# Sink heads: probabilities divided by VectorE ahead of their transposes, and the transposes around the values put in another order

## The chip, the cores and the metric

One core of a Trainium2 chip runs the whole kernel in one launch. The metric is the device time of one execution in microseconds (us). The core has a matmul engine (TensorE, PE in the profile, with its weight loads as PEld), three engines for elementwise work (VectorE or DVE, ScalarE or ACT, GpSimd or POOL) and a queue for transfers (SyncE, SP). They run side by side, each through its own list of instructions in order, and wait for each other by semaphores.

## The reference

Two layers over 256 tokens of width 1024, all in float32. Each layer is a half-weighted SwiGLU block, an attention block and a second half-weighted SwiGLU block. The attention block has two kinds of heads on one input projection. The A heads, with which the change deals, have a learned sink logit:

```python
m = jnp.maximum(jnp.max(scores, axis=-1, keepdims=True), sink_l)
e = jnp.exp(scores - m)
p = e / (jnp.sum(e, axis=-1, keepdims=True) + jnp.exp(sink_l - m))
out = jnp.einsum('bnkgqj,bnjkd->bnqkgd', p.astype(v.dtype), vb)
```

There are eight A query heads on two key heads; with 256 tokens and a window of 128 the band is written as a mask over all 256 keys. The four B heads are differential attention (one softmax less lambda times another) with a norm behind it, which takes any common factor out again. Both outputs go through one output projection.

## The kernel before

Everything is cut into tiles of 128 rows. Weights are read from memory as blocks of 1 MB, a few smaller (`raw`), and split by ScalarE and VectorE into a high and a low part in TensorE's rounded format (`w`: ScalarE copies, VectorE subtracts, `emit_split`, L207); a product is then three matmuls of 128x512: high by high, low by high, high by low (`tokens`). The order of splits relative to the matmuls is set by the numbers in `LEAD` (L32): at each place where the program takes the next block (`weights`, L273, and `ahead`, L244), a number says how many half blocks ahead of it are to be split by then. In the rest of the program the instructions stand as written (`Kept`, L52). In the softmax part of the attention (`kept[0] = False` at L1035 until L1157) the instructions of ScalarE, VectorE and GpSimd are put in order by the scheduler; TensorE's always stand as written, and `urgent` (L100) moves what it encloses forward.

PSUM has six banks for general use (`bank`, L83) and two for pairs (`pair`, L86; `xy` in the profile).

The attention is `mix` (L959). A step of it deals with two rows of heads at once; A steps are numbered 0 to 3 (two of the eight A heads each). `scores` (L986) does 24 short matmuls, then for each half of the queries and each head a VectorE step that adds the bias and takes the row's extremum (`negm`), and a ScalarE exponential with its row sum (`den`). `soft_b` (L1010) joins the two softmaxes of a B head. `soft_a` (L1023) adds the sink to the sum: `es`, its exponential, and `den_a`. It returns the exponentials undivided.

Then the program turns them keys-first: `keys_first` (L1053) does eight transposes on TensorE into two banks, and copies one bank by ScalarE, the other by VectorE. There are two groups for the B heads (`keys_first_b`) and four for the A heads (`keys_first_a`, one for each A step). The matmuls of the B values (`vB`, 48 of 128x512 in a pair of banks) are interleaved: the scores of A steps 0 and 1 behind kk = 1, those of steps 2 and 3 and the second B group behind kk = 4 (L1089). vB is scaled, half by ScalarE, half by VectorE, behind A group 0. Then come the A groups 1 to 3, and the B outputs (32 matmuls of `v` by `s`, into a pair, `osl`).

The A heads' divisor is applied last. The reciprocals of all sums (`ra`, L1105) are spread by GpSimd over 64 columns for each head (`rw`), transposed by TensorE four at a time (`turn_sums`, L1112), copied by ScalarE, and multiplied by VectorE into the output `oa`, which 16 matmuls of 64x256 have just made of the transposed exponentials and `vA`; the product `t_` is split into `oT` (L625). This happens twice (`cp`), for two groups of heads each. `norm_b` (L1129) brings the B outputs to the same form, and `out_part` multiplies `oT` by the output weights.

Of the kernel before, what the change touches and what calls it, by code (L numbers as in the profile page):

```python
# [9 lines left out]
F32 = mybir.dt.float32  # L10
F32R = mybir.dt.float32r
AF = mybir.ActivationFunctionType
ALU = mybir.AluOpType

P = 128
# [13 lines left out]
N_RAW, N_S4 = 6, 28  # L29
IN_FFN, IN_MIX = 8, 6  # L30
SEVEN = ((2, 3, 4), (1, 2, 3, 4))
LEAD = dict(start=(5, 7, 10, 10),  # L32
            open0=(2, 0, 0, 2, 6, 6, 8, 6, 5, 6, 1, 10, 2, 5, 7, 7, 8, 0),
            first=(1, 1, 1, 7, 12, 15, 16, 19, 19, 22, 22),
            mid=(2, 8, 12, 12, 15, 15, 20, 20, 20, 22, 23),
            last=(1, 7, 12, 14, 15, 15, 17, 20, 20, 21, 22),
            mid0=(6, 9, 12, 14, 15, 15, 19, 19, 19, 22, 24),
            last0=(2, 8, 12, 13, 15, 15, 19, 20, 20, 23, 25),
            first0=(2, 3, 3, 4, 7, 11, 11, 14, 14, 18, 18),
            open=(8, 12, 11, 9, 11, 11, 9, 5),  # L40
            close0=(7, 5, 7, 5, 6, 10, 3, 10, 5, 11, 4, 7, 1),
            close=(1, 8, 9, 9, 6, 8, 8, 9, 1, 7, 5, 4, 6),
            mix=(10, 2, 0, 2, 9, 2, 3, 5, 6, 11, 5, 2, 3, 1, 6, 5, 2, 4, 1, 6, 7, 8, 6, 11, 7, 8))


@with_exitstack
def trunk(ctx: ExitStack, tc: tile.TileContext, x, n1, g1, u1, d1, nm, w_in, sink,
# [21 lines left out]
    pe, act, dve, pool = Kept(nc.tensor, True), Kept(nc.scalar), Kept(nc.vector), Kept(nc.gpsimd)  # L69
# [30 lines left out]
    def urgent():  # L100

        return tc.high_priority(300)
# [402 lines left out]
    norm = Norm(0)  # L505

    def take_x(k):
# [15 lines left out]
        elif k == 1.25:  # L523
            norm.pair(2)
            norm.squares(1, 0, 512)
            ahead(LEAD["start"][0])
        elif k == 1.5:
# [157 lines left out]
    def ffn(norm, aside=None, before=None, final=False, sevens=SEVEN[1]):  # L685
# [57 lines left out]
        def by_sevens(h, groups, old):  # L743
# [215 lines left out]
    def mix(l, norm, nxt_norm):  # L959
        kbs = {}  # L960
        den_b = tmp("den_b", 1, (P, HB, 4))
        den_a = tmp("den_a", 1, (P, 4, 4))
# [60 lines left out]
        def soft_a(c, q):  # L1023
            ns = nsnk[:, l, c].rearrange("p t s -> p (t s)")
            den = den_a[:, c]
            e, negm = scores(q, kbs["a"], distA, [slopeA[c], slopeA[c + 4]], [ns[:, n:n + 1] for n in range(4)], den)
            es = tmp("es", 4, (P, 4))
            dve.tensor_tensor(es, negm, snk[:, l, c].rearrange("p t s -> p (t s)"), op=ALU.add)
            act.activation(es, es, AF.Exp)
            dve.tensor_tensor(den, den, es, op=ALU.add)  # L1030
            return e


# [12 lines left out]
        vsl = halves(bank())  # L1046
# [6 lines left out]
        def keys_first(pick):  # L1053

            out_ = blk(F32)
            for kc in range(2):
                tsl = bank()
                for i in range(4):
                    pe.transpose(tsl[:, i * P:(i + 1) * P], pick(kc, i), ident)
                (act.copy if kc == 0 else dve.tensor_copy)(out_[:, kc], tsl)  # L1060
            return out_

        def keys_first_b(hp):
            return keys_first(lambda kc, i: a_b[2 * hp + i // 2][:, i % 2, kc * P:(kc + 1) * P])

        def keys_first_a(c):
            return keys_first(lambda kc, i: p_a[c][:, i % 2, (i // 2) * 256 + kc * P:(i // 2) * 256 + (kc + 1) * P])


        aT = [keys_first_b(0)]  # L1070
        vB = tp.tile([P, 2, 512], F32, tag="v", bufs=1, name=nm_("v"))
        both = pair()
        vsl = both
        for k0 in (0, 4):
            w = weights()
            for k in range(4):
                kk = k0 + k
                hi, lo = w.part(k)
                xv = norm.xs[kk // 2][:, kk % 2]
                for t in range(2):  # L1080
                    xh, xl = xv[:, t * P:(t + 1) * P], xv[:, S + t * P:S + (t + 1) * P]
                    pe.matmul(vsl[t], lhsT=xh, rhs=hi, start=kk == 0, stop=False)
                    pe.matmul(vsl[t], lhsT=xl, rhs=hi, start=False, stop=False)
                    pe.matmul(vsl[t], lhsT=xh, rhs=lo, start=False, stop=kk == KC - 1)
                if kk == 1:
                    p_a = [soft_a(0, qA0[0]), soft_a(1, qA0[1])]
                elif kk == 4:
                    p_a += [soft_a(2, qA1[0]), soft_a(3, qA1[1])]
                    aT.append(keys_first_b(1))  # L1089
        pT = [keys_first_a(0)]  # L1090
        act.activation(vB[:, 0], vsl[0], AF.Copy, scale=norm.r[:, 0:1])
        dve.tensor_scalar_mul(vB[:, 1], vsl[1], norm.r[:, 1:2])
        for c in range(1, 4):
            pT.append(keys_first_a(c))

        def turned(o, cp, sl):

            for c in range(2):
                for t in range(2):
                    pe.transpose(sl[:, c * 256 + t * P:c * 256 + (t + 1) * P],  # L1100
                                 o[:, t, (2 * cp + c) * P:(2 * cp + c + 1) * P], ident)
            return halves(sl)


        ra = tmp("ra", 1, (P, 4, 4))  # L1105
        dve.reciprocal(ra, den_a)
        rw = blk(F32)
        for t in range(2):
            pool.tensor_copy(rw[:, t].rearrange("p (c a d) -> p c a d", c=4, a=2),
                             ra[:, :, 2 * t:2 * t + 2].unsqueeze(3).to_broadcast([P, 4, 2, 64]))  # L1110

        def turn_sums(cp):  # L1112
            turned(rw, cp, rsl[cp])
            rT = tmp()
            act.copy(rT, halves(rsl[cp]))
            return rT


        oT = [blk() for _ in range(4)]
        rsl, both = [bank() for _ in range(2)], pair()  # L1120
        osl = both
        for t in range(2):
            for h in range(HB):
                for kc in range(2):
                    c0 = (h % 2) * 256 + t * P
                    pe.matmul(osl[t][:, h * P:(h + 1) * P], lhsT=aT[h // 2][:, kc, c0:c0 + P],
                              rhs=vB[:, kc, h * P:(h + 1) * P], start=kc == 0, stop=kc == 1)

        def norm_b():  # L1129

# [28 lines left out]
        next(of_b)  # L1159
        oa = [halves(bank()) for _ in range(2)]  # L1160
        for cp in range(2):
            rT = turn_sums(cp)
            for c in range(2):
                for kc in range(2):
                    for a in range(2):
                        pp = slice(a * 64, a * 64 + 64)
                        pe.matmul(oa[cp][pp, c], lhsT=vA[:, kc, pp], rhs=pT[2 * cp + c][:, kc, a * 256:a * 256 + 256],
                                  start=kc == 0, stop=kc == 1)
            t_ = tmp()
            if cp:  # L1170
                next(of_b)
            dve.tensor_tensor(t_, oa[cp], rT, op=ALU.mult)
            split(oT[cp], t_)


        accs = [[bank(), bank()] for _ in range(2)]
# [35 lines left out]
    for l in range(DEPTH):  # L1212
# [7 lines left out]
        if not final:  # L1220
            norm = Norm((l + 1) * 8)
# [76 lines left out]
```

## Time and profile before

| what | before |
|---|---|
| median of three runs | 911.79 us (911.65 to 912.84) |
| the profiled execution | 912.2 us |
| its span, first to last instruction | 910.4 us |
| TensorE busy | 902.3 us |
| VectorE busy | 777.5 us |
| ScalarE busy | 613.8 us |
| granted TensorE clock, mean | 0.998 |
| attention of layer 0, A and B softmax to output projection | about 198 to 281 us of the span |
| attention of layer 1 | about 645 to 728 us |

The busy times are of the one profiled execution; the instructions of an engine overlap a little, so the differences of starts in a list by time are a better measure of what a group takes than the durations in it. In the profile nearly all lines read L62, since a helper there issues the instructions, and one goes by tiles: `ident,s` are transposes, `s,vA` the A outputs, `v,s` the B outputs, `w,s` products with weights.

### The profile page before, as it was taken

Reading aid. Unit: us, or ns where it says so; the run is one execution under the profiler, and the core shown is the slowest. Engines: PE = TensorE matmul, PEld = TensorE weight load, DVE = VectorE, ACT = ScalarE, POOL = GpSimd, SP = SyncE. Lnnn points to the kernel's source line nnn. Section 1 sums busy time; section 2 is a strip of 40 time slices with the busy share of each in tenths; the row PEclk is TensorE's granted clock in tenths of the full one; section 3 lists DMA queues with packets and bytes.
Section 4 is the critical chain, followed back from the end, with each engine's and each line's share of the span. In section 5 each row is a group of like instructions: output and inputs, shape, how many; then the busy total and the mean of one; then the engine's idle time right before and its main releaser. Section 6 shows DMA issues by size and latency. Waiting matters only on the chain.

```text
span 910.4 us, 12060 instructions
## 1 busy us (share of the span) xinstructions
PE 902.3 (99%) x4486; PEld 754.2 (83%) x4486; DVE 777.5 (85%) x1053; ACT 613.8 (67%) x975; POOL 64.9 (7%) x83
## 2 busy tenths in 40 slices
PE   9999999999999999999999999999999999999997
PEld 8888888888888888888888888888888888888886
DVE  5859999879876899999778999997896878999894
ACT  6856677677776766677575776676766686776660
POOL 0411000000001001000000101000001000101011
PEclk9999999999999999999999999999999999999999
DMA  9998897956048788897966898897720786898731
GB/s 331 336 271 235 232 317 249 266 141 224 1 145 236 176 269 247 239 306 249 304 186 163 254 282 265 238 303 214 219 98 1 256 215 176 235 311 250 222 114 47
DMA packets 114060, 200.83 MB, mean 221 GB/s; under 512 B 3663, under 2 KB 31377, under 8 KB 114001
## 3 DMA queue, kind: packets, MB, share of 16 engines
q1 hardware_dynamic: 97344, 167.53, 54.1%
q0 software_dynamic: 16096, 31.75, 20.1%
q8 instruction: 35, 0.57, 0.3%
q10 hardware_dynamic: 560, 0.79, 0.3%
q14 instruction: 25, 0.20, 0.1%
HBM read 199.00 MB, written 1.05 MB: 220 GB/s over the span
## 4 chain that ended last, share of the span: by engine, by line
PE 91%; DMA 5%; DVE 1%; ACT 1%; issue 1%; POOL 0%; SPq 0%; POOLq 0%; ACTq 0%
PE ps L62 69%; PE xy L62 22%; DMA raw<-in_ffn_w_up_dram 4%; DVE w L62 1%; DMA raw<-in_ffn_w_gate_dram 1%; ACT w L62 1%; ACT junk L62 0%; POOL r L62 0%; ACT s L62 0%; DVE s L62 0%; ACT tmp L62 0%; SPq L172 0%; DVE xk L62 0%; DVE q L62 0%; POOLq L1293 0%
## 5 line engine op out<-in xcount | busy, mean ns | idle before, releaser
L62 DVE TENSOR_TENSOR w<-raw,w 128x1024 fp32r<-128x1024 f32 (+1 forms) x458 | 476.7, 1099 | 36.1 <-ACT w L62 35.1
L62 PE MATMUL ps<-w,s 128*128 128x512 f32 (+1 forms) x2046 | 473.7, 389 | 0.3 <-DVE s L62 0.3
L62 ACT CAST w<-raw 128x1024 fp32r<-128x1024 f32 (+1 forms) x458 | 405.0, 953 | 60.6 <-DVE raw L62 40.9
L62 PEld LDWEIGHTS ps<-w,s 128*128 128x128 f32 x2046 | 380.2, 188 | 78.7 <-ACT tmp L62 0.8
L62 PE MATMUL xy<-w,s 128*128 128x512 f32 x528 | 125.7, 391 | 0.0
L62 PEld LDWEIGHTS xy<-w,s 128*128 128x128 f32 x528 | 98.3, 188 | 20.3
L62 PE MATMUL xy<-w,q 128*128 128x512 f32 x360 | 88.1, 393 | 0.0
L62 PEld LDWEIGHTS xy<-w,q 128*128 128x128 f32 x360 | 66.5, 188 | 13.2
L62 PE MATMUL ps<-s,w 128*128 128x512 f32 (+1 forms) x384 | 70.2, 339 | 0.0
L62 POOL DMA_DIRECT2D raw<-in_ffn_w_up_dram x30 | 38.9, 1315 | 432.6 <-DVE w L62 262.6
L62 DVE TENSOR_TENSOR raw<-raw,raw 128x2048 f32<-128x2048 f32 x30 | 68.7, 2289 | 0.5
L62 PEld LDWEIGHTS ps<-s,w 128*128 128x128 f32 x384 | 58.9, 188 | 8.4
L62 ACT ACTIVATE s<-ps,gcol 128x256 fp32r<-128x256 f32 (+1 forms) x80 | 31.4, 478 | 38.3 <-PE ps L62 38.3
L62 PE MATMUL ps<-w,q 128*128 128x512 f32 x180 | 43.2, 389 | 0.0
L62 PE MATMUL ps<-w,v 128*128 128x512 f32 x180 | 43.2, 389 | 0.0
L62 ACT CAST s<-ps 128x512 fp32r<-128x512 f32 x32 | 18.1, 593 | 36.5 <-PE ps L62 36.3
L62 PEld LDWEIGHTS ps<-w,q 128*128 128x128 f32 x180 | 33.8, 188 | 7.0
L62 PEld LDWEIGHTS ps<-w,v 128*128 128x128 f32 x180 | 33.8, 188 | 7.0
L62 DVE TENSOR_TENSOR s<-ps,s 128x512 fp32r<-128x512 f32 x32 | 21.3, 688 | 18.0 <-ACT s L62 17.9
L62 ACT ACTIVATE s<-s,negm 128x256 f32<-128x256 f32 x64 | 31.7, 498 | 6.1 <-DVE negm L62 6.0
L62 PE MATMUL ps<-ident,s 128*128 128x128 f32 x256 | 34.0, 273 | 0.0
L62 PEld LDWEIGHTS ps<-ident,s 128*128 128x128 f32 x256 | 29.7, 140 | 4.8 <-issue 0.8
(128 smaller groups left out, 557.2 us busy)
## 6 DMA issues: line engine op xcount, KB each, us to landing
raw<-in_ffn_w_down_dram SPq DMA_DIRECT2D x44, 1024.0 KB, 7.3
raw<-in_ffn_w_gate_dram SPq DMA_DIRECT2D x39, 1024.0 KB, 7.4
raw<-in_ffn_w_up_dram SPq DMA_DIRECT2D x39, 1024.0 KB, 7.1
raw<-in_ffn_w_up_dram POOLq DMA_DIRECT2D x30, 1024.0 KB, 9.8
raw<-in_w_in_dram SPq DMA_DIRECT2D x14, 1024.0 KB, 7.7
raw<-in_ffn_w_gate_dram SPq DMA_DIRECT2D x8, 512.0 KB, 8.0
raw<-in_ffn_w_up_dram SPq DMA_DIRECT2D x8, 512.0 KB, 9.0
raw<-in_w_in_dram SPq DMA_DIRECT2D x8, 512.0 KB, 6.8
```

The source lines that it names most:

```text
L62: ins = issue(*a, **k)
```

## The change

1. `soft_a` divides the exponentials itself: a reciprocal of the four sums of two heads (into `es`) and one VectorE product of 128x1024 with these four numbers broadcast along 256 columns each, in place.
2. `ra`, `rw`, `turn_sums` and the product with `rT` go away; `split` reads the A output in PSUM.
3. The second B group of transposes moves from behind kk = 4 to behind the last matmul of vB; vB's scaling becomes urgent and stands ahead of it; A groups 0 and 1 follow, then the B outputs, then A groups 2 and 3.
4. Ten of the twelve rows of `LEAD` change, in one to eighteen of their numbers each. One of these rows, and the rest of the diff:

```diff
-            mix=(10, 2, 0, 2, 9, 2, 3, 5, 6, 11, 5, 2, 3, 1, 6, 5, 2, 4, 1, 6, 7, 8, 6, 11, 7, 8))
+            mix=(10, 0, 0, 0, 11, 3, 2, 6, 8, 9, 5, 1, 3, 0, 3, 5, 2, 2, 4, 5, 4, 8, 1, 10, 4, 9))
...
             dve.tensor_tensor(den, den, es, op=ALU.add)
+            dve.reciprocal(es, den)
+            ev = e.rearrange("p t (a n) -> p (t a) n", a=2)
+            dve.tensor_tensor(ev, ev, es.unsqueeze(2).to_broadcast([P, 4, 256]), op=ALU.mult)
             return e
...
                     p_a += [soft_a(2, qA1[0]), soft_a(3, qA1[1])]
-                    aT.append(keys_first_b(1))
+        with urgent():
+            act.activation(vB[:, 0], vsl[0], AF.Copy, scale=norm.r[:, 0:1])
+            dve.tensor_scalar_mul(vB[:, 1], vsl[1], norm.r[:, 1:2])
+        aT.append(keys_first_b(1))
         pT = [keys_first_a(0)]
-        act.activation(vB[:, 0], vsl[0], AF.Copy, scale=norm.r[:, 0:1])
-        dve.tensor_scalar_mul(vB[:, 1], vsl[1], norm.r[:, 1:2])
-        for c in range(1, 4):
-            pT.append(keys_first_a(c))
+        pT.append(keys_first_a(1))
...
-        ra = tmp("ra", 1, (P, 4, 4))
-        dve.reciprocal(ra, den_a)
-        rw = blk(F32)
-        for t in range(2):
-            pool.tensor_copy(rw[:, t].rearrange("p (c a d) -> p c a d", c=4, a=2),
-                             ra[:, :, 2 * t:2 * t + 2].unsqueeze(3).to_broadcast([P, 4, 2, 64]))
-
-        def turn_sums(cp):
-            turned(rw, cp, rsl[cp])
-            rT = tmp()
-            act.copy(rT, halves(rsl[cp]))
-            return rT
...
+        for c in (2, 3):
+            pT.append(keys_first_a(c))
...
         for cp in range(2):
-            rT = turn_sums(cp)
...
-            t_ = tmp()
             if cp:
                 next(of_b)
-            dve.tensor_tensor(t_, oa[cp], rT, op=ALU.mult)
-            split(oT[cp], t_)
+            split(oT[cp], oa[cp])
```

How TensorE's list changes in layer 0, from the B outputs on. The names carry buffer numbers; `xy` are the B outputs, `vA` the A outputs, `ident` the transposes. Before, from the last transposes of A group 3:

```order
L62 MATMUL ps_468_2490<-ident_72,s4_452_2403 128x128 x4
L62 MATMUL ps_469_2496<-ident_72,s4_452_2403 128x128 x4
L62 MATMUL xy_478_2513<-v_430_2266,s4_427_2253 128x128 x4
L62 MATMUL xy_478_2513<-v_430_2266,s4_455_2417 128x128 x4
L62 MATMUL xy_479_2514<-v_430_2266,s4_427_2253 128x128 x4
L62 MATMUL xy_479_2514<-v_430_2266,s4_455_2417 128x128 x4
L62 MATMUL ps_476_2511<-ident_72,s4_471_2504 128x128 x4
L62 MATMUL ps_485_2543<-s4_458_2448,vA_422_2206 64x256 x4
L62 MATMUL ps_485_2543<-s4_461_2463,vA_422_2206 64x256 x4
L62 MATMUL ps_477_2512<-ident_72,s4_471_2504 128x128 x4
L62 MATMUL ps_486_2544<-s4_464_2476,vA_422_2206 64x256 x4
L62 MATMUL ps_486_2544<-s4_467_2489,vA_422_2206 64x256 x4
```

And with the change, from the B outputs on:

```order
L62 MATMUL xy_466_2482<-v_425_2252,s4_422_2239 128x128 x4
L62 MATMUL xy_466_2482<-v_425_2252,s4_453_2439 128x128 x4
L62 MATMUL xy_467_2483<-v_425_2252,s4_422_2239 128x128 x4
L62 MATMUL xy_467_2483<-v_425_2252,s4_453_2439 128x128 x4
L62 MATMUL ps_469_2501<-ident_72,s4_445_2373 128x128 x4
L62 MATMUL ps_470_2507<-ident_72,s4_445_2373 128x128 x4
L62 MATMUL ps_472_2514<-ident_72,s4_450_2403 128x128 x4
L62 MATMUL ps_473_2520<-ident_72,s4_450_2403 128x128 x4
L62 MATMUL ps_479_2538<-s4_456_2452,vA_417_2192 64x256 x4
L62 MATMUL ps_479_2538<-s4_459_2465,vA_417_2192 64x256 x4
L62 MATMUL ps_480_2539<-s4_468_2500,vA_417_2192 64x256 x4
L62 MATMUL ps_480_2539<-s4_471_2513,vA_417_2192 64x256 x4
```

The transposes of the spread reciprocals (`s4_471_2504` before) are gone, and A groups 2 and 3 stand behind the B outputs.

VectorE's list in layer 0, behind the score steps of A steps 2 and 3. Before, `s4_455` is the copy of the second B group, `v` the scaled half of vB and the other copies those of the A groups:

```order
L62 TENSOR_TENSOR es_449_2385<-negm_448_2376,snk_114 128x4
L62 COPY s4_455_2417<-ps_457_2424 128x512
L62 TENSOR_TENSOR es_454_2413<-negm_453_2404,snk_114 128x4
L62 TENSOR_TENSOR den_a_335_1709<-den_a_335_1709,es_449_2385 128x4
L62 TENSOR_TENSOR den_a_335_1709<-den_a_335_1709,es_454_2413 128x4
L62 RECIPROCAL ra_470_2502<-den_a_335_1709 128x16
L62 TENSOR_SCALAR v_430_2266<-xy_432_2268,r_354_1794 128x512
L62 COPY s4_458_2448<-ps_460_2455 128x512
```

With the change, `s4_430`, `s4_435` and `s4_445` are the exponentials of A steps 0, 1 and 2, and `s4_453` is the copy of the second B group:

```order
L62 RECIPROCAL es_432_2291<-den_a_337_1715 128x4
L62 RECIPROCAL es_437_2321<-den_a_337_1715 128x4
L62 TENSOR_TENSOR es_452_2413<-negm_451_2404,snk_114 128x4
L62 TENSOR_TENSOR s4_430_2281<-s4_430_2281,es_432_2291 128x1024
L62 TENSOR_TENSOR s4_435_2311<-s4_435_2311,es_437_2321 128x1024
L62 TENSOR_TENSOR den_a_337_1715<-den_a_337_1715,es_447_2383 128x4
L62 TENSOR_TENSOR den_a_337_1715<-den_a_337_1715,es_452_2413 128x4
L62 TENSOR_SCALAR v_425_2252<-xy_427_2254,r_354_1794 128x512
L62 RECIPROCAL es_447_2383<-den_a_337_1715 128x4
L62 COPY s4_453_2439<-ps_455_2446 128x512
L62 RECIPROCAL es_452_2413<-den_a_337_1715 128x4
L62 TENSOR_TENSOR s4_445_2373<-s4_445_2373,es_447_2383 128x1024
```

The copy of the second B group, which stood ahead of the sums of steps 2 and 3, now stands behind two products, vB's half and a reciprocal.

On the same engine, between the scores of A steps 0 and 1 and those of 2 and 3 (the scheduler's place for the first two pairs of output weight subtractions, which stood earlier before):

```order
L62 TENSOR_TENSOR es_432_2291<-negm_431_2282,snk_114 128x4
L62 TENSOR_TENSOR w_439_2328<-raw_326_1648,w_438_2327 128x512 x2
L62 TENSOR_TENSOR es_437_2321<-negm_436_2312,snk_114 128x4
L62 TENSOR_TENSOR w_441_2334<-raw_326_1648,w_440_2333 128x512 x2
L62 ISA s4_445_2373,negm_446_2374<-ps_443_2359,distA_111,nsnk_116 128x256
```

The pair `w_439` and the pair `w_441` are now in this gap; before, only the adds of es and den stood there.

More of the change, by code (lines that the diff above doesn't have):

```diff
@@ L31 @@
 SEVEN = ((2, 3, 4), (1, 2, 3, 4))
-LEAD = dict(start=(5, 7, 10, 10),
-            open0=(2, 0, 0, 2, 6, 6, 8, 6, 5, 6, 1, 10, 2, 5, 7, 7, 8, 0),
-            first=(1, 1, 1, 7, 12, 15, 16, 19, 19, 22, 22),
+LEAD = dict(start=(2, 7, 8, 6),
+            open0=(2, 0, 0, 2, 3, 6, 8, 6, 5, 6, 1, 10, 1, 5, 7, 6, 8, 0),
+            first=(1, 1, 2, 8, 12, 15, 16, 19, 19, 22, 22),
             mid=(2, 8, 12, 12, 15, 15, 20, 20, 20, 22, 23),
             last=(1, 7, 12, 14, 15, 15, 17, 20, 20, 21, 22),
[L37 to L42, printed above, removed]
-            mix=(10, 2, 0, 2, 9, 2, 3, 5, 6, 11, 5, 2, 3, 1, 6, 5, 2, 4, 1, 6, 7, 8, 6, 11, 7, 8))
+            mid0=(4, 9, 12, 15, 15, 15, 19, 19, 19, 22, 24),
+            last0=(2, 8, 12, 13, 15, 15, 19, 20, 20, 22, 25),
+            first0=(0, 0, 3, 6, 6, 11, 11, 11, 12, 18, 18),
+            open=(10, 11, 9, 7, 11, 11, 9, 5),
+            close0=(6, 3, 7, 5, 6, 10, 3, 10, 5, 11, 4, 6, 1),
+            close=(0, 8, 9, 9, 6, 2, 7, 6, 1, 10, 5, 4, 8),
+            mix=(10, 0, 0, 0, 11, 3, 2, 6, 8, 9, 5, 1, 3, 0, 3, 5, 2, 2, 4, 5, 4, 8, 1, 10, 4, 9))
 @with_exitstack
@@ L1102, in turned @@
             return halves(sl)
-        ra = tmp("ra", 1, (P, 4, 4))
-        dve.reciprocal(ra, den_a)
-        rw = blk(F32)
-        for t in range(2):
-            pool.tensor_copy(rw[:, t].rearrange("p (c a d) -> p c a d", c=4, a=2),
-                             ra[:, :, 2 * t:2 * t + 2].unsqueeze(3).to_broadcast([P, 4, 2, 64]))
-        def turn_sums(cp):
-            turned(rw, cp, rsl[cp])
-            rT = tmp()
-            act.copy(rT, halves(rsl[cp]))
-            return rT
         oT = [blk() for _ in range(4)]
-        rsl, both = [bank() for _ in range(2)], pair()
+        both = pair()
         osl = both
```

## The prediction

> **What bounds the kernel now.** I read the page's engine table first, then the slices, then the chain that ended last, and then TensorE in order of time where the change works.
>
> ```profile
> PE 902.3 (99%) x4486; PEld 754.2 (83%) x4486; DVE 777.5 (85%) x1053; ACT 613.8 (67%) x975; POOL 64.9 (7%) x83
> ...
> PE   9999999999999999999999999999999999999997
> ...
> PE 91%; DMA 5%; DVE 1%; ACT 1%; issue 1%; POOL 0%; SPq 0%; POOLq 0%; ACTq 0%
> ```
>
> TensorE is busy in every slice but the last and holds 91% of the chain. A busy TensorE need not be one without gaps, so the waits count more: its own list has two entries, and only the second is inside the work.
>
> ```profile
> PE ps L62 <- POOL ident masks.py:199: 1.4, 1, 1.4
> PE ps L62 <- DVE s L62: 0.3, 1, 0.3
> ```
>
> So from about 6 us on, time goes away only where TensorE has less to do, and comes back only where it is made to wait. VectorE, at 85%, has room on average; what matters is whether it is late at a place where TensorE asks for its result. These are the rows of TensorE in the attention of layer 0 (columns: start, duration of the merged group, engine, line, operation, tiles, shapes, count):
>
> ```profile
> 233.57 1.69 PE L62 MATMUL ps<-s,q 64*128 64x256 f32 x24
> 235.19 4.37 PE L62 MATMUL xy<-w,s 128*128 128x512 f32 x18
> 239.49 1.69 PE L62 MATMUL ps<-s,q 64*128 64x256 f32 x24
> 241.11 1.09 PE L62 MATMUL ps<-ident,s 128*128 128x128 f32 x8
> 241.96 4.37 PE L62 MATMUL xy<-w,s 128*128 128x512 f32 x18
> 246.16 3.65 PE L62 MATMUL ps<-ident,s 128*128 128x128 f32 x32
> 249.65 3.74 PE L62 MATMUL xy<-v,s 128*128 128x128 f32 x32
> 253.22 0.60 PE L62 MATMUL ps<-ident,s 128*128 128x128 f32 x4
> 253.75 1.95 PE L62 MATMUL ps<-s,vA 128*64 128x256 f32 x16
> 255.63 0.66 PE L62 MATMUL ps<-ident,s 128*128 128x128 f32 x4
> 256.22 1.95 PE L62 MATMUL ps<-s,vA 128*64 128x256 f32 x16
> 258.09 5.74 PE L62 MATMUL ps<-w,s 128*128 128x512 f32 x24
> ```
>
> Each group starts where the one before it ends (the durations overlap a little, so I take differences of starts). The two groups of four transposes at 253.22 and 255.63 are the reciprocals' own; the change deletes them.
>
> **The gain.** 253.75 - 253.22 = 0.53 us and 256.22 - 255.63 = 0.59 us, 1.12 us in layer 0. In layer 1 the same four rows give 0.53 and 0.58:
>
> ```profile
> 700.37 0.60 PE L62 MATMUL ps<-ident,s 128*128 128x128 f32 x4
> 700.90 1.95 PE L62 MATMUL ps<-s,vA 128*64 128x256 f32 x16
> 702.78 0.66 PE L62 MATMUL ps<-ident,s 128*128 128x128 f32 x4
> 703.36 1.95 PE L62 MATMUL ps<-s,vA 128*64 128x256 f32 x16
> ```
>
> Together **2.2 us**, and that is nearly all that can be had: by the bare spacing of transposes, (249.65 - 246.16) / 32 = 0.109 us, the 16 deleted ones are 1.7 us, and the rest is the change from one kind of matmul to another. All other transposes keep their number and only change places. The Trainium skill, TensorE: Matmul & The Clock Gate, Part 4 (PE-mode transpose), has a 128x128 transpose at about 275 ns in a kernel's context. By that the 16 would be worth 4.4 us and the kernel would end near 907.4; the trace's starts, 0.109 us apart, speak against it, and I leave it out of the sum.
>
> **What the edits on other engines cost.** ScalarE loses four copies and GpSimd four, VectorE four products of 512 and two reciprocals of 16; nobody on TensorE's path misses them. The split of each A output now reads PSUM itself, which takes one VectorE step out between the values' matmuls and the output projection. VectorE gains eight products of 128x1024 and eight reciprocals of 4. No row before has that product in place with a broadcast factor. Its floor is 1.14 us (two 1024 subtractions in a row take 2.36), the group's mean is 1.22, and a broadcast factor costs nothing in the one row that has one (682 against 685 ns for plain products of 512):
>
> ```profile
> L62 DVE TENSOR_TENSOR w<-raw,w 128x1024 fp32r<-128x1024 f32 x354 | 411.6, 1220 | 31.0 <-ACT w L62 30.1
> ...
> L62 DVE TENSOR_TENSOR tmp<-s,tmp 128x512 f32<-128x512 f32 x8 | 5.5, 685 | 0.0
> ...
> L62 DVE TENSOR_TENSOR s<-xy,rb 128x512 f32<-128x512 f32 x4 | 2.6, 682 | 0.0
> ...
> L62 DVE RECIPROCAL rc<-den_b 128x2 f32<-128x2 f32 x8 | 1.3, 159 | 0.6 <-ACT s L62 0.6
> ```
>
> I take 1.18 each in a row of two, 1.14 as the lower end and 2.29 as the upper one (the 128x2048 additions' mean, as if the broadcast halved the rate). Eight of them are 9.4 us of VectorE time, and they count only where TensorE waits.
>
> **The added wait, followed in layer 0.** TensorE's transposes of an A step now wait for that step's product, and the B outputs' matmuls (`xy<-v,s`) stand directly behind two such groups. The VectorE rows of before give the steps:
>
> ```profile
> 232.85 1.29 DVE L62 TENSOR_TENSOR w<-raw,w 128x512 fp32r<-128x512 f32 x2
> ...
> 237.90 0.28 DVE L62 TENSOR_TENSOR es<-negm,snk 128x4 f32<-128x4 f32 x2
> ...
> 240.50 0.48 DVE L62 CUSTOM_DVE_ANT_0 s<-ps,distA,nsnk 128x256 f32<-128x256 f32 x1 [0.89 <-PE ps L62]
> ...
> 243.75 0.16 DVE L62 TENSOR_TENSOR es<-negm,snk 128x4 f32<-128x4 f32 x1
> ...
> 245.68 0.26 DVE L62 TENSOR_TENSOR den_a<-den_a,es 128x4 f32<-128x4 f32 x2 [1.11 <-ACT es L62]
> 245.97 0.25 DVE L62 RECIPROCAL ra<-den_a 128x16 f32<-128x16 f32 x1
> 246.36 0.75 DVE L62 TENSOR_SCALAR v<-xy,r 128x512 f32<-128x512 f32 x1
> 247.23 0.69 DVE L62 COPY s<-ps 128x512 f32<-128x512 f32 x1
> ```
>
> The changed order puts two pairs of weight subtractions behind the scores of A steps 0 and 1 (at 237.90). A pair is 1.21 (1.29 less the overlap with its follower), so with the two small adds VectorE comes to steps 2 and 3 at 237.90 + 2 x 1.21 + 0.28 = 240.6. TensorE delivered those scores only at 240.50, so these splits are covered by a wait of 0.89 that VectorE had anyway. From there: eight VectorE passes over the scores 3.25 (240.50 to 243.75), two adds of den 0.26, two es and two reciprocals 0.6, which is 244.7; two products 2.36, 247.05; two adds 0.26; the scaled half of vB 0.75, 248.05; one reciprocal 0.16; the copy of the second pair of B heads' transposes 0.69, **248.9**.
>
> TensorE: from 241.11 eighteen matmuls of vB, 4.30 (the step from 235.19 to 239.49), to 245.4; three groups of eight transposes (second B group, A steps 0 and 1) at 0.87 each. Step 0 is asked for at 246.3 and ready at about 245.9; step 1 is asked for at 247.15 and ready at 247.05; the B outputs start at 248.0 and need vB at 248.05. Their sixth matmul, due at 248.0 + 5 x 0.11 = 248.55, needs the copy that ends at 248.9. That, with a little for vB, is a wait of some **0.4 us**; queued behind it are the other B outputs, the last transposes and the output projection, so TensorE loses it whole.
>
> Behind it there is room. Step 2's product is done by 250.3 and asked for at 252.0; step 3's by 252.2 against 252.9. The A output's split ends near 257.0 against a projection due at 257.5. The weights of the second output slice, which before were split ahead of the softmax and now after the second output, are done near 261.1 and wanted near 263.5. The ScalarE side is early too: its exponentials for steps 2 and 3 end near 245.5 (before, at 245.37), and their sums are added at 247.05 only.
>
> Layer 1 has the same VectorE order and the same rows 447.1 us later, so it pays the same 0.4.
>
> **Elsewhere** the table of numbers moves a split past a few rows at the start and at the ends of the FFNs. The one place where TensorE had no margin is this:
>
> ```profile
> 69.81 8.23 PE L62 MATMUL ps<-w,s 128*128 128x512 f32 x35 [0.26 <-DVE s L62]
> ```
>
> In the changed order `hr`, which needs GpSimd's result at 25.9, stands one subtraction earlier in VectorE's queue, so the buffers of 24 to 29 us come free about 0.2 late; 0.26 could turn into 0.5, or vanish. I take nothing and keep 0.3 either way. The loads that start later fall into a stretch in which the DMA stood still:
>
> ```profile
> 230.00:260.00 30.00, 30.00 (x225) 24.92 (x224) 21.34 (x66) 17.80 (x54) 2.81 (x3) 1.00 0.00 1
> ```
>
> (last two columns: DMA share, GB/s). They cost nothing.
>
> **Sum.** -2.2 + 2 x 0.4 + 0 = **-1.4 us**. The profiled execution took 912.2 (its span of 910.4 and 1.8 around it), which gives 910.8; the median of the runs shown is 911.79, and from it 910.4. I forecast **910.4**.
>
> **Rivals.**
>
> *No wait at all.* If VectorE reaches the copy half a microsecond sooner (products at 1.14, adds of den overlapped), TensorE never stops: 911.8 - 2.2 = 909.6. For it: every step above is read with its full duration. Against: the copy stands behind seven VectorE steps that all need the scores of steps 2 and 3 done.
>
> *A wait in place of the deleted work.* If the same chain is 0.7 us later than I have it (each same-engine wait of a reciprocal for its sum, and of a product for its reciprocal, costs a little), steps 0 and 1 are late as well and the wait per layer is 1.1: the gain is given back, 911.8. For it: step 1 has 0.1 of margin and vB none.
>
> *Slower: the broadcast product runs at half rate.* At 2.29 the first two products end 2.2 later, so step 1, vB and the copy are late by that, and step 3's product comes 1.4 after TensorE asks for it: 0.4 + 2.2 + 1.4 = 4.0 of wait against 1.12 saved, 2.9 in each layer, 917.6. It loses from about 1.55 us per product on. Against it are the 682 ns of the broadcast row; for it, that this form (in place, three dimensions, factor of stride zero) is in no row.
>
> That the change doesn't do what it says is excluded by the order: the sixteen transposes, the copies and the spread are gone.
>
> **How the numbers follow.** Forecast 45% (own range 909.8 to 911.2, by 0.15 in each layer's wait and 0.3 at the start), no wait 25%, gain given back 22%, half rate 8%. The range takes in the first three with their spread and leaves out the fourth and the ends: 909.2 to 912.4. A measurement of this kernel can tell about 0.2% (1.8 us) from no change. Faster by more than that, below 910.0: the no-wait case and the lowest 7 in 100 of the forecast, 0.32. Slower, above 913.6: half rate and 2 in 100 of the third case, 0.10. Within: 0.58.
>
> **What would show it.** The rows of `ident,s` x4 between the `s,vA` groups are gone and `s,vA` is one group of 32 in about 3.6 us. The products `s<-s,es` 128x1024 have a mean near 1.2. TensorE's list of waits names VectorE's `s` (the copy) or `v` with about 0.4 each in two places, inside or just ahead of `xy<-v,s`. If instead its starts there are seamless, the first rival holds; if it waits ahead of the transposes of A steps too, the second; if the products' mean is over 1.55, the third. A new TensorE wait in the FFNs would mean that the table's moved splits were mis-read.

## The result, and the profile after

| what | before | changed |
|---|---|---|
| median | 911.78 us (911.53 to 912.84, 11 runs) | 909.68 us (909.18 to 910.43, 11 runs) |
| ratio, with its 95% interval | | 0.9976 (0.9967 to 0.9984) |
| span of the profiled execution | 910.4 us | 907.9 us |
| TensorE busy | 902.3 us | 900.1 us |
| VectorE busy | 777.5 us | 784.2 us |

The changed kernel is 2.1 us faster, 0.24%. It is the first rival of the prediction, no wait at all, which gave 909.6, and not the forecast of 910.4. The time lies just below the forecast's own range (909.8 to 911.2); it is inside the stated range because that takes in the first rival too.

The list of TensorE's waits in the changed kernel has one entry, the one at the very start:

```profile
PE ps L62 <- POOL ident masks.py:199: 1.4, 1, 1.4
```

An empty list is not yet proof (an experiment below loses 0.8 us with the same list), so I go by starts. These are TensorE's rows of the changed kernel in the attention of layer 0, to hold against those in the prediction:

```profile
233.31 1.69 PE L62 MATMUL ps<-s,q 64*128 64x256 f32 x24
234.93 4.37 PE L62 MATMUL xy<-w,s 128*128 128x512 f32 x18
...
247.69 3.74 PE L62 MATMUL xy<-v,s 128*128 128x128 f32 x32
251.26 1.91 PE L62 MATMUL ps<-ident,s 128*128 128x128 f32 x16
253.10 3.67 PE L62 MATMUL ps<-s,vA 128*64 128x256 f32 x32
256.71 5.74 PE L62 MATMUL ps<-w,s 128*128 128x512 f32 x24
262.28 1.03 PE L62 MATMUL ps<-ident,s 128*128 128x128 f32 x8
```

From the first scores to the output projection it is 256.71 - 233.31 = 23.40 us, before 258.09 - 233.57 = 24.52: **1.12 us** less, what the two deleted groups of transposes took. The B outputs take 251.26 - 247.69 = 3.57 as before (253.22 - 249.65), so nothing waits inside them. Layer 1 gives 702.72 - 679.33 = 23.39 against 705.24 - 680.72 = 24.52, 1.13. Before:

```profile
680.72 1.69 PE L62 MATMUL ps<-s,q 64*128 64x256 f32 x24
...
705.24 5.74 PE L62 MATMUL ps<-w,s 128*128 128x512 f32 x24
```

And with the change:

```profile
679.33 1.69 PE L62 MATMUL ps<-s,q 64*128 64x256 f32 x24
...
702.72 5.74 PE L62 MATMUL ps<-w,s 128*128 128x512 f32 x24
```

That is 2.25 us; the other 0.25 of the spans' difference of 2.5 has arisen by about 78 us (the next group of TensorE starts at 77.87 before and at 77.62 with the change), and the experiments show that it lies within what starts differ by from execution to execution.

VectorE's rows of the changed kernel from the end of the score passes on show why nothing waits:

```profile
243.64 0.15 DVE L62 TENSOR_TENSOR es<-negm,snk 128x4 f32<-128x4 f32 x1
243.72 0.23 DVE L62 RECIPROCAL es<-den_a 128x4 f32<-128x4 f32 x2
243.87 0.13 DVE L62 TENSOR_TENSOR es<-negm,snk 128x4 f32<-128x4 f32 x1
243.92 2.36 DVE L62 TENSOR_TENSOR s<-s,es 128x1024 f32<-128x1024 f32 x2
246.20 0.23 DVE L62 TENSOR_TENSOR den_a<-den_a,es 128x4 f32<-128x4 f32 x2
246.34 0.74 DVE L62 TENSOR_SCALAR v<-xy,r 128x512 f32<-128x512 f32 x1
247.01 0.17 DVE L62 RECIPROCAL es<-den_a 128x4 f32<-128x4 f32 x1
247.09 0.66 DVE L62 COPY s<-ps 128x512 f32<-128x512 f32 x1
```

The copy for which I forecast the wait ends at 247.75, which is 248.0 on the scale of before (this trace is 0.26 earlier here), against 248.9 forecast. The product's group, by shape, has the mean that was forecast, so the half-rate rival is out:

```profile
L62 DVE TENSOR_TENSOR s<-s,es 128x1024 f32<-128x1024 f32 x8 | 9.5, 1212 | 0.0
```

### The profile page after: what moved, and what is told of

Same layout as the page of the kernel before. It is cut to its first block, busy times and chain, and to the rows that moved or that the text cites. A ratio compares the mean times of both kernels' runs of the same rounds, so it can differ in the third digit from the quotient of the medians.

```text
span 907.9 us, 12028 instructions
## 1 busy us (share of the span) xinstructions
PE 900.1 (99%) x4470; PEld 753.0 (83%) x4470; DVE 784.2 (86%) x1063; ACT 610.9 (67%) x971; POOL 63.5 (7%) x79
## 3 DMA queue, kind: packets, MB, share of 16 engines
HBM read 199.00 MB, written 1.05 MB: 220 GB/s over the span
## 4 chain that ended last, share of the span: by engine, by line
PE 99%; issue 0%; DVE 0%; POOL 0%; POOLq 0%
PE ps L62 73%; PE xy L62 25%; DVE s L62 0%; DVE xk L62 0%; POOLq L1282 0%; POOL rf L62 0%; POOL ident masks.py:199 0%; POOL ident masks.py:197 0%; DVE tot L62 0%; POOLq masks.py:199 0%; DVE tmp L62 0%; POOLq L1273 0%
## 5 line engine op out<-in xcount | busy, mean ns | idle before, releaser
L62 ACT CAST s<-ps 128x512 fp32r<-128x512 f32 x36 | 20.4, 592 | 44.0 <-PE ps L62 43.8
L62 DVE TENSOR_TENSOR s<-ps,s 128x512 fp32r<-128x512 f32 x36 | 24.1, 688 | 20.5 <-ACT s L62 20.4
L62 ACT COPY ps<-ps 128x512 f32<-128x512 f32 x15 | 8.6, 570 | 34.6 <-PE ps L62 34.6
L62 PE MATMUL ps<-ident,s 128*128 128x128 f32 x240 | 31.4, 272 | 0.0
```

The source lines that it names most:

```text
L62: ins = issue(*a, **k)
```

## The experiments

The kernel before ran beside each of them; its medians were 911.78 to 912.22.

### The table of numbers alone, both ways

The first is the changed kernel with all numbers of before (one row shown):

```diff
-            mix=(10, 0, 0, 0, 11, 3, 2, 6, 8, 9, 5, 1, 3, 0, 3, 5, 2, 2, 4, 5, 4, 8, 1, 10, 4, 9))
+            mix=(10, 2, 0, 2, 9, 2, 3, 5, 6, 11, 5, 2, 3, 1, 6, 5, 2, 4, 1, 6, 7, 8, 6, 11, 7, 8))
...
```

> The changed kernel with the numbers of before in its table. Theory A (the gain is the deleted transposes, 2.24 us of TensorE, plus a wait of about 0.25 at 69.8 us that the table removed): the wait at 69.8 comes back, the attention stays seamless, the span is 908.2 against 907.9 for the changed kernel, the time about 910.0. With the old numbers VectorE does the first two products ahead of the scores of A steps 2 and 3; by the rows of the changed kernel the copy for the B outputs then ends near 248.1 on that kernel's scale, due 248.24. Theory B (the seamless attention needs the new numbers, which put weight subtractions there): TensorE waits 0.4 to 1.1 us in each layer, span 908.9 to 910.4, time 910.7 to 912.2.

The second is the kernel before with the new numbers:

> The kernel before with the numbers of the changed kernel in its table, nothing else. Theory A: only the wait of 0.26 at 69.8 us goes, span 910.1 to 910.2, time about 911.5. Theory B (the table is worth a good part of the gain): span below 909.5, time below 911.0.

Measured: 909.46 us (ratio 0.9974, 0.9964 to 0.9984), span 908.2, for the changed kernel with the old numbers; 911.89 us (0.9999, 0.999 to 1.0008), span 910.3, for the kernel before with the new ones. The old numbers leave the attention seamless:

```profile
233.38 1.69 PE L62 MATMUL ps<-s,q 64*128 64x256 f32 x24
...
256.77 5.74 PE L62 MATMUL ps<-w,s 128*128 128x512 f32 x24
```

23.39 us, so theory B falls: the table is worth nothing that these runs can tell. Nor did the copy for the B outputs come late with the old numbers: it ends at 247.41 (246.73 + 0.68), not near 248.1. But theory A was wrong on the start: the wait at 69.8 us did not come back with the old numbers. In this kernel TensorE's group there starts at 69.52 and is one piece of 36 matmuls, which in the first trace of before was cut in two by the wait:

```profile
69.52 8.32 PE L62 MATMUL ps<-w,s 128*128 128x512 f32 x36
```

### Both kernels once more, for the start

> The kernel before once more, for one look at its start. Theory F (the wait of 0.26 at 69.8 us belongs to that one execution: its start was 0.3 us quicker than that of all other traces, and the wait gave this back): start of the first value projection slower than 7.46, no wait at 69.8, the A outputs' group at the same distance from the start. Rival (the wait belongs to the order of before): the wait of 0.26 again.

> The changed kernel once more, for one look at its start. Theory F: no wait at 69.8, span 907.9 within the 0.3 to 0.6 us by which starts differ from execution to execution; 23.4 us from the scores of steps 0 and 1 to the output projection, as in its first trace.

Measured, in one execution of each: spans of 910.8 and 908.5, and 257.21 - 233.82 = 23.39 us from the scores to the projection in the changed kernel, as in its first trace. The second group of products at the start, and the group at 69.9, in TensorE's rows of the kernel before, run again:

```profile
8.26 1.53 PE L62 MATMUL xy<-w,s 128*128 128x512 f32 x6
...
69.94 8.32 PE L62 MATMUL ps<-w,s 128*128 128x512 f32 x36
```

The second group starts at 8.26 here, and there is no wait at 69.9. In the first trace of before the group started at 7.46, in that of the changed kernel at 7.75. Before, in the first trace:

```profile
7.46 1.53 PE L62 MATMUL xy<-w,s 128*128 128x512 f32 x6
```

The start differs by up to 0.8 us from execution to execution of the same kernel. Only the trace with the quickest start has the wait at 69.8, and no run of either table with a slower one has it. By the starts it cost 0.55 us there: from 69.16 to the next group at 77.87 is 8.71, and in the run of the changed kernel with the old numbers 77.68 - 69.52 = 8.16.

The quick start is only half of it. In that trace a load of weights also came late. ScalarE's split of it starts at 59.96, the latest of all traces, and VectorE's part for which TensorE waits ends at 69.75. In the run of the changed kernel with the old numbers these are 58.84 and 68.64, which is ahead even of the first trace's 69.16. Whether the old numbers have a part in the late load is open: they give 58.84 to 59.96 in five traces, the new ones 57.82 to 59.36 in nine.

So the 0.25 can't be called an effect of the change: the group behind the wait starts anywhere from 77.4 to 78.3 in the fourteen traces of all runs, and at 78.10 and 78.12 in these two. These two executions happen to start alike (8.26 and 8.27), and their spans differ by 2.3, the two layers' 2.25. What makes the start vary was not tested.

### Only the transposes taken out

The kernel before, whose A outputs are multiplied by the untransposed reciprocals:

```diff
-            turned(rw, cp, rsl[cp])
-            rT = tmp()
-            act.copy(rT, halves(rsl[cp]))
-            return rT
+            return rw[:, cp].rearrange("p (a n) -> p a n", a=2)
```

> The kernel before without the sixteen transposes of the spread reciprocals and the four ScalarE copies behind them; the A outputs are multiplied by the spread reciprocals as they stand, untransposed, so these outputs are not the reference's. Theory A: the group of 16 value matmuls follows the other at once, 1.12 us less in each layer, span 908.2 (the wait at 69.8 stays), time 909.6. Theory C (the new order of transposes is a gain in itself, or the deleted groups' steps were partly a cost of switching between kinds of matmul that stays): less than 1.6 us in all, span above 908.8.

Measured: 910.62 us (0.9985, 0.9976 to 0.9994), span 908.8. Theory A fails by 0.6 us of span and 1.0 of time, and the list of TensorE's waits has the start's entry only. The rows of this kernel tell where it went:

```profile
233.46 1.69 PE L62 MATMUL ps<-s,q 64*128 64x256 f32 x24
...
253.21 3.67 PE L62 MATMUL ps<-s,vA 128*64 128x256 f32 x32
256.81 6.14 PE L62 MATMUL ps<-w,s 128*128 128x512 f32 x24
262.79 1.03 PE L62 MATMUL ps<-ident,s 128*128 128x128 f32 x8
```

Up to the projection it is 23.35 us, as short as in the changed kernel. But the 24 matmuls of the projection take 262.79 - 256.81 = 5.98 in place of 5.57 (262.28 - 256.71). The list of all engines in order of time, with the weight loads (PEld), has a wait for VectorE's `s` there and not among the matmuls:

```profile
255.27 0.69 DVE L62 TENSOR_TENSOR tmp<-ps,s 128x512 f32<-128x512 f32 x1 [0.36 <-PE ps L62]
256.00 0.62 ACT L62 CAST s<-tmp 128x512 fp32r<-128x512 f32 x1 [2.09 <-DVE tmp L62]
256.65 0.69 DVE L62 TENSOR_TENSOR s<-tmp,s 128x512 fp32r<-128x512 f32 x1 [0.68 <-ACT s L62]
256.81 0.19 PEld L62 LDWEIGHTS ps<-w,s 128*128 128x128 f32 x1 [0.39 <-ACT s L62]
...
257.39 0.77 PEld L62 LDWEIGHTS ps<-w,s 128*128 128x128 f32 x4 [0.40 <-DVE s L62]
```

The first A output goes through three steps (product, high part, low part) before the projection can use it, and the low part ends at 257.34, when TensorE has been there since 256.81. It is the second entry, 0.40, that costs the 0.41; the 0.39 ahead of the first weight load costs nothing, since the changed kernel has 0.38 at the same place. In the kernel before, the second group of transposes hid these steps: the low part ended at 257.88 (257.19 + 0.69), and the projection came at 258.09. In the changed kernel, without the product, it ends at 256.40 (255.71 + 0.69), and the projection comes at 256.71. A new theory, E: the product behind the A outputs, hidden before, costs 0.4 us in each layer as soon as the transposes go.

### The step put back, and the step taken out

The changed kernel with one VectorE pass in the product's place:

```diff
-            split(oT[cp], oa[cp])
+            t_ = tmp()
+            dve.tensor_copy(t_, oa[cp])
+            split(oT[cp], t_)
```

> The changed kernel with a VectorE copy (128x512, out of PSUM into SBUF) put back between each A output and its split, where the kernel before had its product. Theory E (the 0.4 us in each layer that the kernel without the transposes lost in the output projection is this step's, once no transposes stand between the two groups of A outputs): the 24 matmuls of the projection take 5.95 to 6.0 us from first to next group in place of 5.57, the attention is 0.4 longer in each layer, span 908.7 plus the spread of the start, time 910.5. Rival (the loss there was another, such as the wait of the product for the spread reciprocals): projection 5.57, time 909.7.

And the kernel before with neither transposes nor that product:

```diff
-            rT = turn_sums(cp)
...
-            dve.tensor_tensor(t_, oa[cp], rT, op=ALU.mult)
-            split(oT[cp], t_)
+            split(oT[cp], oa[cp])
```

> The kernel before without the sixteen transposes and without the products of the A outputs, which are split straight out of PSUM; the A outputs stay undivided, so they are not the reference's. It has neither the new order of transposes nor products of probabilities. Theory E: the attention is 1.12 us shorter in each layer, like the changed kernel, projection 5.57, span 908.2 by the start's spread, time 909.6 to 909.8. Rival (the new order of transposes has a part in the gain): 0.8 or less in each layer, time above 910.2.

Measured: 910.98 us (0.999, 0.9981 to 0.9999), span 908.9, with the extra pass; 909.77 us (0.9975, 0.9965 to 0.9985), span 908.0, without either. With the extra pass:

```profile
256.56 0.50 PE L62 MATMUL ps<-w,s 128*128 128x512 f32 x1
257.29 5.49 PE L62 MATMUL ps<-w,s 128*128 128x512 f32 x23 [0.22 <-DVE s L62]
262.61 1.03 PE L62 MATMUL ps<-ident,s 128*128 128x128 f32 x8
```

6.05 us for the projection, 0.48 more than the changed kernel's 5.57; from the scores to the projection's end it is 0.53 more (262.61 - 233.11 = 29.50 against 262.28 - 233.31 = 28.97). That is somewhat above the 0.4 expected, as is the time (910.98 against 910.5). Without either step, in the order of before:

```profile
233.44 1.69 PE L62 MATMUL ps<-s,q 64*128 64x256 f32 x24
...
256.80 5.74 PE L62 MATMUL ps<-w,s 128*128 128x512 f32 x24
262.37 1.03 PE L62 MATMUL ps<-ident,s 128*128 128x128 f32 x8
```

23.36 and 5.57: the whole gain, with neither the new order nor the new products. Theory E stands, with 0.4 to 0.5 us in each layer.

### The products left out

```diff
-            dve.tensor_tensor(ev, ev, es.unsqueeze(2).to_broadcast([P, 4, 256]), op=ALU.mult)
```

> The changed kernel without the products of the probabilities (the A outputs stay undivided; reciprocals are still taken). Theory A (products lie wholly beside TensorE's work): span 907.9, time 909.7, within 0.2 of the changed kernel in the span; VectorE's busy time falls by 9 to 10 us. Theory D (something of the added wait is there, inside rows that look seamless): span 907.1 to 907.5.

Measured: 910.00 us (0.9977, 0.9968 to 0.9986), span 908.2, VectorE busy 776.0 us in place of 784.2. From the scores to the projection it is 23.39 us:

```profile
233.65 1.69 PE L62 MATMUL ps<-s,q 64*128 64x256 f32 x24
...
257.04 5.74 PE L62 MATMUL ps<-w,s 128*128 128x512 f32 x24
```

The 0.3 of span is the start again (233.65 against 233.31). The products cost TensorE nothing. VectorE's busy time falls by 8.2 us, less than the 9 to 10 expected; why was not followed up.

### The products twice

```diff
             dve.tensor_tensor(ev, ev, es.unsqueeze(2).to_broadcast([P, 4, 256]), op=ALU.mult)
+            dve.tensor_tensor(ev, ev, es.unsqueeze(2).to_broadcast([P, 4, 256]), op=ALU.mult)
```

> The changed kernel with each product of the probabilities issued twice (the A outputs are divided twice). It is the rival in which the product runs at half rate. By the rows of the changed kernel, with 1.14 us for each further product: A step 0 is ready at 247.5 against 245.94 asked, step 1 waits 0.95 more, steps 2 and 3 together 1.2: a wait of 3.7 us in each layer, span 915.3, time 917.2. The recorded rival had 4.0 of wait in each layer. Rival theory (products have more cover than the chain shows, for example because transposes are asked for later): below 2 us in each layer, time below 913.7.

Measured: 918.43 us (1.0069, 1.0055 to 1.0083), span 916.6. TensorE:

```profile
235.00 4.37 PE L62 MATMUL xy<-w,s 128*128 128x512 f32 x18
...
247.78 1.06 PE L62 MATMUL ps<-ident,s 128*128 128x128 f32 x8 [1.60 <-DVE s L62]
249.57 1.94 PE L62 MATMUL ps<-ident,s 128*128 128x128 f32 x8 [0.73 <-DVE es L62]
...
260.99 5.28 PE L62 MATMUL ps<-w,s 128*128 128x512 f32 x22
```

260.99 - 235.00 = 25.99 against 256.71 - 234.93 = 21.78, 4.2 us lost in layer 0 (4.3 in layer 1); a wait of 3.7 was expected, and the prediction's rival with products at half rate had 4.0 and 917.6. (The list stops at 266 us and so shows 22 of the projection's 24.)

Not all of this is a wait. The two groups of transposes with a wait start 1.77 and 0.92 us after the group of eight ahead of them is through (0.87 us each), 2.7 together. The last eight then take 251.30 - 249.57 = 1.73 in place of 0.87, and the B outputs 255.54 - 251.30 = 4.24 in place of 3.57; that is the other 1.5. In this stretch the granted TensorE clock is at 0.50 (the third number from the end of this row for 250 to 251 us):

```profile
250.00:251.00 1.00, 1.00 (x7) 1.00 (x6) 1.00 (x4) 0.31 (x1) 0.00 (x0) 0.50 0.07 16
```

It is 1.00 until 249 and again from 253 us on; in layer 1 it is at 0.50 from 700 to 703. No other trace here has it below 1.00 between 232 and 270 us, also not those below in which TensorE waits once in each layer (1.22 and 1.51 us by its list). What lowers it was not tested.

The waits for steps 0 and 1 are about as expected (1.56 and 0.95); the 1.2 for steps 2 and 3 did not come. An estimate from the rows says why: step 3's product ends at 255.88 (253.54 + 2.34 on VectorE), and without the 1.5 TensorE would have asked for it near 254.9, a wait of 1.0; the slow stretch hides it. So the cover is there but thin: 1.14 us more for each product makes the change a loss.

### The copy late, and a little late

VectorE's copy of the second B group made twice:

```diff
-        def keys_first(pick):
+        def keys_first(pick, times=1):
...
-                (act.copy if kc == 0 else dve.tensor_copy)(out_[:, kc], tsl)
+                for _ in range(times if kc else 1):
+                    (act.copy if kc == 0 else dve.tensor_copy)(out_[:, kc], tsl)
...
-        aT.append(keys_first_b(1))
+        with urgent():
+            aT.append(keys_first_b(1))
```

`keys_first_b` passes 2 as `times` for the second group, and the group becomes `urgent`.

> The changed kernel with VectorE's copy of the second B group made twice; the second one stands behind the product of step 2 and the copy of step 0, so it ends near 250.2 in place of 247.75 in layer 0. Theory A (the sixth matmul of the B outputs, due at 248.24, needs that copy, as forecast, and the forecast only had the copy 0.9 late): a wait of 2.0 us in each layer inside the B outputs' matmuls, named as VectorE's s, span 911.9, time 913.7. Rival (the copy is not what TensorE would wait for): span below 909.

Both halves of vB on VectorE:

```diff
-            act.activation(vB[:, 0], vsl[0], AF.Copy, scale=norm.r[:, 0:1])
+            dve.tensor_scalar_mul(vB[:, 0], vsl[0], norm.r[:, 0:1])
```

> The changed kernel with both halves of the scaled vB on VectorE, none on ScalarE: one step of 0.67 us more ahead of the copy. Theory A (margin of about 0.5 us at the copy, 0.6 at vB): copy ends near 248.4 against 248.24 due, a wait of 0.1 to 0.3 us in each layer, span 908.1 to 908.5, time about 910.1. If the margin were larger than the rows say, no wait; if the forecast's 0.4 of wait were hidden in seamless rows, 0.7 and more in each layer, span above 909.2.

Measured: 912.79 us (1.0009, 1.0 to 1.0018), span 910.9, with the copy twice; 909.81 us (0.9975, 0.9966 to 0.9985), span 908.5, with vB on VectorE. With the copy twice, VectorE makes two copies in a row from 248.88 on, that of A step 0 and the second one of the B group. They end at 248.88 + 1.28 = 250.16, and TensorE waits for that:

```profile
248.88 1.28 DVE L62 COPY s<-ps 128x512 f32<-128x512 f32 x2
```

```profile
247.71 1.28 PE L62 MATMUL xy<-v,s 128*128 128x128 f32 x10
250.21 2.72 PE L62 MATMUL xy<-v,s 128*128 128x128 f32 x22 [1.22 <-DVE s L62]
252.76 1.91 PE L62 MATMUL ps<-ident,s 128*128 128x128 f32 x16
```

So the copy is what TensorE would wait for. But it stops after **ten** rows, not five, and loses 252.76 - 247.71 - 3.57 = 1.48 us in place of 2.0. With vB on VectorE the copy ends 248.70 - 248.04 = 0.66 behind the start of the B outputs, 0.6 later than in the changed kernel (247.75 - 247.69 = 0.06), and costs nothing, where 0.1 to 0.3 were expected; from the scores to the projection it is 23.39 us:

```profile
248.02 0.68 DVE L62 COPY s<-ps 128x512 f32<-128x512 f32 x1
```

```profile
233.67 1.69 PE L62 MATMUL ps<-s,q 64*128 64x256 f32 x24
...
257.06 5.74 PE L62 MATMUL ps<-w,s 128*128 128x512 f32 x24
```

### The old order of transposes with the new division

```diff
-        with urgent():
-            act.activation(vB[:, 0], vsl[0], AF.Copy, scale=norm.r[:, 0:1])
-            dve.tensor_scalar_mul(vB[:, 1], vsl[1], norm.r[:, 1:2])
-        aT.append(keys_first_b(1))
+                    aT.append(keys_first_b(1))
         pT = [keys_first_a(0)]
-        pT.append(keys_first_a(1))
+        act.activation(vB[:, 0], vsl[0], AF.Copy, scale=norm.r[:, 0:1])
+        dve.tensor_scalar_mul(vB[:, 1], vsl[1], norm.r[:, 1:2])
+        for c in range(1, 4):
+            pT.append(keys_first_a(c))
...
-        for c in (2, 3):
-            pT.append(keys_first_a(c))
```

The scaling of vB goes back to its old place with them.

> The changed kernel with the transposes in the order of before: second B group in the middle of vB, all four A steps ahead of the B outputs. Theory A: step 2's product ends near 249.55 against 247.69 asked, step 3's near 250.7 against 250.4: a wait of 2.1 us in each layer, span 912.2, time 914.0; so the new order is what makes the division free. Rival (the order doesn't matter, products are early anyway): span below 908.5, time below 910.3.

Measured: 914.55 us (1.0027, 1.0016 to 1.0037), span 913.1. TensorE:

```profile
233.97 1.69 PE L62 MATMUL ps<-s,q 64*128 64x256 f32 x24
...
246.55 2.17 PE L62 MATMUL ps<-ident,s 128*128 128x128 f32 x16
250.24 2.29 PE L62 MATMUL ps<-ident,s 128*128 128x128 f32 x16 [1.51 <-DVE s L62]
...
259.64 5.74 PE L62 MATMUL ps<-w,s 128*128 128x512 f32 x24
```

25.67 us in place of 23.40, 2.27 in each layer as expected (2.1). Ahead of the B outputs the transposes of steps 2 and 3 wait for their products; behind them they don't. (The wait stands at these transposes and not at vB, whose place has changed too.) The new order, worth nothing by itself, is what makes the division free. No kernel here beats the changed one by more than the noise; the one with the old numbers is as fast.

## Why the prediction held, and which step failed

**The bound and the gain.** TensorE was the bound and stayed it, and the deleted transposes gave 1.12 and 1.13 us, forecast 1.12 and 1.11. Read as differences of starts they came out to within 0.02 us.

**The step that failed** is the added wait: "Their sixth matmul, due at 248.0 + 5 x 0.11 = 248.55, needs the copy that ends at 248.9." Both times were wrong, each by enough to make the 0.4 vanish. The due time: the loops make 16 matmuls (2 x 4 x 2), and the group has 32 rows. Each fp32 matmul of the B outputs stands as two rows, so the sixth one is due ten rows in, at 248.0 + 10 x 0.11 = 249.1; the kernel with the copy twice stopped there. I had taken rows for instructions, though the two counts stood next to each other. (The 32 matmuls of the B outputs and the 16 of each A output in "The kernel before" are rows as well: the lists of order show 16 and 8.) The group shows the price, too: 3.57 / 16 = 0.22 us for a matmul of 128 columns, while the 24 fp32r matmuls of 512 columns in the projection took 5.57 / 24 = 0.23 each. The Trainium skill, FP8 and Floating Point Precision, section TensorE Precision Notes, has true fp32 as four passes through the array; the time agrees if an fp32r matmul is one pass (a quarter of the columns, the same time), the number of rows (two) doesn't show it.

The copy's end: every small step on VectorE was taken with its full duration, and the sums of steps 0 and 1 were counted behind the scores, where they fell between them. From the end of the score passes to the copy's end I had 5.08 us (0.26 + 0.6 + 2.36 + 0.26 + 0.75 + 0.16 + 0.69), and it was 4.11 (243.64 to 247.75); the first of these terms, the sums of steps 0 and 1, stands at 241.87 in the trace. Each step starts some 0.07 before the one ahead of it ends: two reciprocals and two adds of four numbers took 243.92 - 243.64 = 0.28, counted as 0.6; the two sums 0.14 for 0.26; the reciprocal 0.08 for 0.16; the products 2.28 for 2.36; vB 0.67 for 0.75. The Trainium skill, VectorE: DVE Perf Modes, section The DRAIN you can't avoid, says that the next op does not start until the pipe is empty, and that one that is not held starts earlier; the starts here, ahead of the recorded ends, fit the second, though no view shows which op is held. With both errors mended the copy has 248.80 - 247.75 = 1.05 us to spare (247.69 + 10 x 0.111 is due), and vB on VectorE, which used 0.6 of it, cost nothing.

**Costed at nothing.** The products, the splits that moved and the table are free, as forecast. "Nobody on TensorE's path misses them" was wrong of the product behind the A outputs: that it goes is part of the gain. It was hidden before only by the transposes that the change deletes; with them gone and the product kept, 0.4 us are lost in each layer. I had seen that the change takes this step out and gave it no price. It did no harm to the sum, since the change does both, but the gain is of two edits: transposes alone gave 23.35 + 5.98 = 29.33 us from the scores to the end of the projection's group, against 30.10 before (263.67 - 233.57) and 28.97 in the changed kernel.

**The start.** "I take nothing and keep 0.3 either way" held, but not by the reason given: the wait came of that execution's quick start and late load together, and no other trace has it, with either table. Whether the order has a part in the late load is not shown.

**The rivals.** No wait at all (25%) is what happened, for the reason that I gave for it, steps that overlap, and for one that I had missed. Half rate was priced about right in total (4.0 of wait; 4.2 lost with the products twice, which stand in for it), and that the sizes agree so well is luck: its waits ahead of the B outputs were 2.7, there was none for the copy (0.4 in the rival), and the halved clock took 1.5 where the rival had 1.4 for step 3. The gain given back did not happen with this order, and more than that happened with the old one.

## To carry to other kernels

Where the bounding engine has no gaps, price a deletion by differences of starts, and then ask what the deleted work was hiding: here the transposes covered a product on VectorE that would have cost a third of the gain. A due time in a group of matmuls is counted in calls of the code, and the rows per call are counted in the trace first. Work that is added to another engine can be made free by asking for its result later: the order of transposes decided between 0 and 2.3 us in each layer.

## What the runs showed of the hardware

- A wait for the operand of a weight load need not stand in the matmuls' list: 0.40 us on PEld in the kernel without the transposes, with nothing new in TensorE's own list and 0.41 lost by the starts. And where TensorE's list names a wait, more was lost by the starts than it names: 1.51 us named and 2.27 lost with the old order of transposes, 0.22 and 0.48 with the extra pass, 0.26 and 0.55 at 69.8 us in the first trace of before.
- The granted TensorE clock can fall in the middle of a kernel (its mean was 0.998 before): with the products twice it is at 0.50 from 250 to 252 us, right behind two waits (1.60 and 0.73 us by TensorE's list), and eight transposes take 1.73 us in place of 0.87. After a single wait of 1.22 or 1.51 us it stayed at 1.00.
- The product of 128x1024, in place, with a factor broadcast along 256 columns, takes 1.21 us (mean of 8), the same as a plain subtraction of that size (1.22).
- The start of one and the same kernel differs by 0.8 us between executions (7.46 and 8.26 at the second group of products), over a third of what the change is worth.
